# A hybrid encoder block: router in fp32 with tokens on partitions, norm weights applied at the experts' transposes in four parts, convolution evicted behind its last matmul

## The chip, the core and the metric

The kernel is one program on one core of a Trainium2 chip. The metric is device microseconds of one execution. Before the change the median of three runs is 2157.0 us (2156.89 to 2158.53). One further execution was taken with the hardware profiler; its rows are what the document reads.

## The reference, cut to what matters

One encoder layer on 1024 tokens of 1024 channels, all in float32:

```python
h  = rms_norm(x, norm1_g)
z  = h @ w_in                      # columns: q | k | v (512 each), conv a | b (512 each)
attn = dilated_attention(q, k, v)  # 8 heads of 64, three window patterns mixed by their denominators
u  = a * sigmoid(b)
conv = silu(layer_norm(depthwise_conv(u, width 31) + bias))     # 512 channels
x  = x + concat(attn, conv) @ w_out

h   = rms_norm(x, norm2_g)                       # = x * rsqrt(mean(x*x) + eps) * norm2_g
aff = softmax(h @ w_router)                      # 16 experts
gate, idx = top_k(aff.T, 128)                    # each expert chooses its 128 tokens
ye  = (silu(h[idx] @ w1) * (h[idx] @ w3)) @ w2   # per expert, inner width 2816
x   = x + scatter_add(gate * ye, idx)
```

The change touches the depthwise convolution, the second norm with the router, and the place where norm2_g is multiplied in.

## The kernel before, in words

**Number format.** Most products are made of three matmuls in a reduced fp32 format (fp32r in the rows): an operand is split into a high half, rounded on ScalarE, and a low half, the rest, which VectorE or GpSimd subtracts. High times high, high times low and low times high are then summed in PSUM.

**Stages in order.** Until 60 us: loads, the first norm and its splits. 60 to 145 us: the projections for the convolution's two inputs (`z_ab`) and three of the four convolutions. 145 to 300: the projections of q, k and v (`z_pair`, L503), with the fourth convolution at 156 to 171 us. 300 to 447: attention. 447 to 589: the token stage, which makes the output projection, the second norm, the router and the ranking for one block of 128 tokens after another. 589 to 622: the end of the ranking, the search for each expert's tokens, and the first gather. From 622 to the end: sixteen experts of some 94 us each.

**Order of the work.** Each engine works through its own queue in the order in which the kernel issues instructions (`manual_schedule` keeps that order for VectorE, TensorE and ScalarE from the projections to the end). Generators hold back small work and are advanced by hand between other instructions: the ranking's operations are dripped into the token stage, so many at each place, and the glu and the weights' splits are advanced between the convolution's chunks. An instruction that waits holds up what is queued behind it on its engine.

**A convolution** (`conv`) handles 128 of the 512 channels. Its 9 chunks of 4 products with a 128x128 weight run on TensorE over four quarter tiles `ps[:, g]` of 256 columns; one product is three matmuls, and they stand at L362 to L364. Nine products in a row belong to one quarter, so the quarters 0 and 1 are complete in chunk 4. `left(pair)` is ScalarE's eviction of two quarters into the tile `co` with the bias (L341); `to_tokens(pair)` is four 128x128 pieces turned by TensorE into the tile `ct`, then two ScalarE copies into `xn`, tokens on partitions. There is only one `co`, for two quarters, so `left(1)` has to come behind `to_tokens(0)`'s transposes. Before, `left(0)` stands in chunk 4, `to_tokens(0)` at the end of chunk 7, `left(1)` at the end of chunk 8, and `to_tokens(1)` is put in the list `ends`, which `end()` empties between the two parts of the next `z_ab`, or behind the next `z_pair`. Behind the fourth convolution VectorE makes its statistics (`conv_stats`, L377), issued after the token pair that follows, and then rotary rotations and the low halves of the next weights (L407), all in one queue.

**The token stage** (class `Token`, the loop `for t in range(1, NT)`). For a block t: 48 products (`product`) give the output projection, `residual` (L1075, VectorE) adds x, `squares` (L1081, ScalarE) makes the sum of squares, `turned` (L1086) turns the block into eight 128x128 tiles of the transposed x, four in a PSUM tile. ScalarE copies that tile twice: rounded, as the high half, and (L1094) in full into `xf`; GpSimd makes the low half by subtraction (L1095). In the last block VectorE subtracts straight from PSUM. `norm` (L127 to L136) is twelve small VectorE operations for the reciprocal root. `router` (L1116) multiplies with the router's weights as the stationary operand: 128 rows by 32 columns (16 high, 16 low), 128 tokens moving, 16 matmuls into `pr`, experts on partitions. ScalarE copies it to `lT`, `logits` turns it back to tokens on partitions, and VectorE adds the two halves. `softmax` scales by the norm (a ScalarE exponential with a per-token scale), `spread` turns the affinities (L1158) and copies them into the ranking's tile `top`. `kept` makes h for the gather: ScalarE multiplies x by the norm (L1106), GpSimd multiplies by norm2_g, spread over the partitions (`g2`, L1107), and a DMA writes the block to `h2s` in DRAM. The router's weights already hold norm2_g (`router_weights`), so the products take x and not h. The ranking is VectorE's: MAX8 and MATCH_REPLACE runs, then maxima and minima of two SBUF tiles (L989, L991 in `merged`).

**The experts.** For an expert, 128 gathered rows of h (`gather`, an indirect DMA of GpSimd, issued at chunk `GC`) are turned by TensorE (`transposed`, L1417, eight 128x128 pieces in two PSUM tiles) into `xTe`: ScalarE copies a 512-wide tile as the high half (L1419), VectorE subtracts the low half (L1420). That is done at once behind chunk 4 of the expert before. An expert has six chunks of its inner width; each takes two weight tiles for w1, two for w3, and two for w2 (`up`, `down`; the last chunk is half as wide), and each tile is split ahead of use, high half on ScalarE (L1198) and low half on VectorE (L1199). Three high and three low buffers let the splits run three tiles ahead. The products of the chunk before are turned in `h_turned` (L1441).

Of the kernel before, what the change touches and what calls it, by code (L numbers as in the profile page):

```python
# [22 lines left out]
P = 128  # L23
# [4 lines left out]
NE = 16  # L28
# [40 lines left out]
def build(ctx, tc, nc, I, out):  # L69
# [76 lines left out]
    wrr = pack[:, 2 * P:3 * P].rearrange("p (j e) -> p j e", j=8)  # L146
    wr = sm([P, 8, 2, NE], F32R, "wr")
    V.memset(zeros[:, 0, 0:1], 0.0)
# [20 lines left out]
    def router_weights():  # L169
        V.tensor_tensor(wrr, wrr, g2t[:, :, None].to_broadcast([P, 8, NE]), op=ALU.mult)  # L170
        split(wrr, wr[:, :, 0], wr[:, :, 1])

# [161 lines left out]
    def conv(i, ends):  # L334
# [103 lines left out]
    def end():  # L438
        while ends:
            ends.pop(0)()  # L440
# [11 lines left out]
    for i in range(1, 4):  # L452
# [13 lines left out]
        end()  # L466
        z_ab(i, pab, ((1, 1),))
        gates = glu(i, pab[1])
        if i < 3:
# [471 lines left out]
    for n in range(NU + 1):  # L941
# [17 lines left out]
        if n % 4 == 0 and 1 <= h < H - 1:  # L959
# [6 lines left out]
    HW = D + NE  # L966
    misc = slot(4, [D + 2 * P + NT + 2 * NE + 5 * P], F32, "misc")
    g2 = misc[:, 0:D]
    nc.sync.dma_start(g2, I["g2"].partition_broadcast(P))
    cs = misc[:, D:D + 2 * P + NT + 2 * NE]  # L970
# [4 lines left out]
    W, gt, eq = (misc[:, D + 2 * P + NT + 2 * NE + i * P:][:, 0:P] for i in range(3))  # L975
    run = misc[:, D + 5 * P + NT + 2 * NE:].rearrange("p (a k) -> p a k", a=2)
    h2s = dram.tile([S, HW], F32, name="h2s")
# [53 lines left out]
    h22 = slot(10, [2, HW], F32, "h22")  # L1031

    xf = misc[:, D + 2 * P + NT + 2 * NE:][:, 0:512]
    h2T = slot(11, [2, 8, P], F32R, "h2T")
    ORDER = (0, 1, 4, 5, 2, 6, 7, 3)

    class Token:


        def __init__(self, t):  # L1040
            self.t, self.xt, self.h2, self.h2T = t, xt2[:, t % 2], h22[:, t % 2], h2T
            nc.sync.dma_start(self.xt, x_v[:, t])
# [40 lines left out]
        def turned(self, j0, j1, between=None):  # L1083
            pt, n = psT("hT2"), (j1 - j0) * P
            for j in range(j0, j1):
                T.transpose(pt[:, (j - j0) * P:(j - j0 + 1) * P], self.xt[:, j * P:(j + 1) * P], ident)  # L1086
            hh, hl = (self.h2T[:, i, j0:j1].rearrange("p j t -> p (j t)") for i in range(2))
            A.activation(hh, pt[:, 0:n], AF.Copy)
            if between:
                between()  # L1090
            if self.last:
                V.tensor_tensor(hl, pt[:, 0:n], hh.bitcast(F32), op=ALU.subtract)
            else:
                A.activation(xf[:, 0:n], pt[:, 0:n], AF.Copy)  # L1094
                G.tensor_tensor(hl, xf[:, 0:n], hh.bitcast(F32), op=ALU.subtract)  # L1095

# [8 lines left out]
        def scaled(self):  # L1105
            A.activation(self.h2[:, 0:D], self.xt, AF.Copy, scale=self.r)  # L1106
            G.tensor_tensor(self.h2[:, 0:D], self.h2[:, 0:D], g2, op=ALU.mult)  # L1107

        def router(self, j0=0, j1=8):

            if j0 == 0:
                self.pr = psM("pr")
            for part in range(2):
                for j in range(j0, j1):
                    w_ = wr[:, j].rearrange("p a e -> p (a e)")
                    T.matmul(self.pr[0:2 * NE, 0:P], w_, self.h2T[:, part, j], start=j == 0 and not part,  # L1116
                             stop=j == 7 and part == 1)
            if j1 == 8:
                self.lT = pack[0:2 * NE, (3 + self.t % 2) * P:(4 + self.t % 2) * P]
                A.activation(self.lT, self.pr[0:2 * NE, 0:P], AF.Copy)  # L1120

        def logits(self):
            pl = psM("pl")
            T.transpose(pl[:, 0:2 * NE], self.lT, ident[0:2 * NE, 0:2 * NE])
            self.lg = lg = sm([P, NE], F32, "lg", tag="lg", bufs=2)
            self.sc = sm([P, 4], F32, "rsc", tag="rsc", bufs=2)
            V.tensor_copy(lg, pl[:, 0:NE])
            yield
            V.tensor_tensor(lg, pl[:, NE:2 * NE], lg, op=ALU.add)
            yield  # L1130
            V.tensor_reduce(self.sc[:, 0:1], lg, axis=AX.X, op=ALU.max)

        def softmax(self, between=lambda: None, prev=None):
            sc = self.sc
            af = sm([P, NE], F32, "af", tag="af", bufs=2)
            V.tensor_scalar(sc[:, 1:2], sc[:, 0:1], self.r, -1.0, op0=ALU.mult, op1=ALU.mult)
            A.activation(af, self.lg, AF.Exp, scale=self.r, bias=sc[:, 1:2], accum_out=sc[:, 2:3])
            between()
# [272 lines left out]

    def transposed(e, xe):
        xT = slot(XT[e % 2], [2, 8, P], F32R, "xTe")
        for q in range(2):
            pt = psT("xeT")
            for j in range(4):
                T.transpose(pt[:, j * P:(j + 1) * P], xe[:, (4 * q + j) * P:(4 * q + j + 1) * P], ident)  # L1417
            hh = xT[:, 0, 4 * q:4 * q + 4].rearrange("p j t -> p (j t)")
            A.activation(hh, pt, AF.Copy)  # L1419
            V.tensor_tensor(xT[:, 1, 4 * q:4 * q + 4].rearrange("p j t -> p (j t)"), pt, hh.bitcast(F32),  # L1420
                            op=ALU.subtract)
        G.tensor_copy(gate[:, e:e + 1], xe[:, D + e:D + e + 1])
        return xT

# [98 lines left out]
def layouts(inputs):  # L1523
# [6 lines left out]
    L["g1"] = c(f["norm1_g"].reshape(8, P).T)  # L1530
    L["g2"] = c(f["norm2_g"].reshape(1, D))
    L["g2t"] = c(f["norm2_g"].reshape(8, P).T)
# [65 lines left out]
```

## Time and profile before

| | us |
|---|---|
| median of three runs | 2157.0 (2156.89 to 2158.53) |
| the profiled execution's own time | 2155.56 |
| its span | 2153.8 |
| TensorE busy in the span (PE) | 2078.4, 97% |
| its weight loads (PEld) | 1744.8, 81% |
| VectorE (DVE) | 1748.8, 81% |
| ScalarE (ACT) | 1398.6, 65% |
| GpSimd (POOL) | 216.9, 10% |
| high halves of the experts' weights, L1198 (ACT), 530 of 1913 ns mean | 1006.3 |
| low halves, L1199 (DVE), 530 of 2281 ns mean | 1200.6 |

In the rows an instruction is given as its line, engine, operation, the tile it writes, the tile it reads, and the two shapes (partitions x elements). `<-DVE xt L1075` behind an idle time or a wait names what ended it: VectorE's write of the tile `xt` at line 1075. PEld is TensorE's loading of weights, which runs beside its matmuls. The busy share is a mean over stages with different limits, so stretches are read one by one. The chain of waits is followed back from the last instruction of the span, at each step to what released it.

### The profile page before, as it was taken

The page shows a single profiled execution, that of the slowest core. Times are in us where ns is not written, and L with a number is a line of the kernel's source. Part 1 is how long each engine was busy: PE and PEld are TensorE (multiplying, and loading weights), DVE is VectorE, ACT ScalarE, POOL GpSimd, SP SyncE. Part 2 cuts the span into 40 slices and gives each one's busy share as a digit, 9 for nine tenths or more (in the row PEclk, how much of TensorE's full clock was granted, in tenths as well). Part 3 has the DMA queues.
Part 4 walks back from the last instruction along what each step waited for, and adds up shares of the span by engine and source line. Part 5 has one row for each costly group of instructions (what it writes and reads, how often), then busy time and mean ns, then how long its engine had stood idle before and what let it go on. Part 6 is the DMA issues. An engine that isn't in the chain of part 4 may idle for free.

```text
span 2153.8 us, 27850 instructions
## 1 busy us (share of the span) xinstructions
PE 2078.4 (97%) x10458; PEld 1744.8 (81%) x10458; DVE 1748.8 (81%) x2235; ACT 1398.6 (65%) x1463; POOL 216.9 (10%) x164
## 2 busy tenths in 40 slices
PE   9999999998769999999999999999999999999997
PEld 7888889976558888888888888888888888888886
DVE  6346737869968888898898889889888888988885
ACT  5245745553347777777777777777777777777774
POOL 2110001333210100011010101101010100101010
PEclk9999999999979999999999999999999999999998
DMA  8461077744569999999999999999999999999990
GB/s 301 113 170 42 18 170 157 161 141 167 208 248 348 368 386 380 380 375 371 384 363 386 380 380 377 372 380 363 390 378 381 378 368 380 362 388 378 375 354 10
DMA packets 138743, 647.71 MB, mean 301 GB/s; under 512 B 47984, under 2 KB 52464, under 8 KB 68592
## 3 DMA queue, kind: packets, MB, share of 16 engines
q1 hardware_dynamic: 130688, 617.48, 76.9%
q0 software_dynamic: 7776, 28.45, 4.8%
q8 instruction: 82, 1.34, 0.2%
q14 instruction: 53, 0.43, 0.1%
q10 hardware_dynamic: 144, 0.00, 0.0%
HBM read 607.69 MB, written 21.40 MB: 292 GB/s over the span
## 4 chain that ended last, share of the span: by engine, by line
PE 84%; DVE 6%; issue 1%; ACT 1%; DMA 1%; POOL 0%; POOLq 0%; DVEq 0%; ACTq 0%
PE w L113 15%; PE w L115 15%; PE w L114 15%; PE y L115 8%; PE y L113 7%; PE y L114 7%; PE pqk L503 4%; PE po L837 2%; PE pv L503 2%; PE hT L1441 2%; PE pp L817 1%; PE sc L778 1%; DVE top L991 1%; PE sc L779 1%; DVE top L989 1%
## 5 line engine op out<-in xcount | busy, mean ns | idle before, releaser
L1199 DVE TENSOR_TENSOR w<-rw,w 128x2048 fp32r<-128x2048 f32 (+1 forms) x530 | 1200.6, 2281 | 185.0 <-ACT w L1198 180.8
L1198 ACT ACTIVATE w<-rw 128x2048 fp32r<-128x2048 f32 (+1 forms) x530 | 1006.3, 1913 | 274.8 <-PE w L115 138.9
L113 PE MATMUL w<-w,xTe 128*128 128x512 f32 (+1 forms) x1536 | 584.4, 380 | 0.0
L115 PE MATMUL w<-w,xTe 128*128 128x512 f32 (+1 forms) x1536 | 574.8, 374 | 0.0
L114 PE MATMUL w<-w,xTe 128*128 128x512 f32 (+1 forms) x1536 | 574.4, 374 | 0.0
L115 PEld LDWEIGHTS w<-w,xTe 128*128 128x128 f32 x1536 | 289.1, 188 | 54.6 <-DVE xTe L1420 0.2
L114 PEld LDWEIGHTS w<-w,xTe 128*128 128x128 f32 x1536 | 289.8, 189 | 51.5
L113 PEld LDWEIGHTS w<-w,xTe 128*128 128x128 f32 x1536 | 289.4, 188 | 51.1 <-ACT xTe L1419 0.4
L115 PE MATMUL y<-w,hts 128*128 128x512 f32 x700 | 276.8, 395 | 0.0
L113 PE MATMUL y<-w,hts 128*128 128x512 f32 x700 | 275.4, 393 | 0.0
L114 PE MATMUL y<-w,hts 128*128 128x512 f32 x700 | 275.0, 393 | 0.0
L114 PEld LDWEIGHTS y<-w,hts 128*128 128x128 f32 x700 | 131.9, 188 | 30.7
L113 PEld LDWEIGHTS y<-w,hts 128*128 128x128 f32 x700 | 131.9, 188 | 29.1
L115 PEld LDWEIGHTS y<-w,hts 128*128 128x128 f32 x700 | 131.8, 188 | 29.2
L1443 ACT ACTIVATE hts<-hT 128x512 fp32r<-128x512 f32 x95 | 53.8, 566 | 112.5 <-PE hT L1441 112.5
L1477 POOL DMA_INDIRECT out_dram<-xy,idx x16 | 74.4, 4651 | 422.8 <-DVE xy L1476 343.4
L1408 POOL DMA_INDIRECT xy<-h2s,idx x16 | 17.6, 1102 | 895.3 <-PE xeT L1417 683.3
L503 PE MATMUL pqk<-wqkv,hT 128*128 128x512 f32 x384 | 89.6, 394 | 0.0
L503 PEld LDWEIGHTS pqk<-wqkv,hT 128*128 128x128 f32 x384 | 72.1, 188 | 16.5
L164 DVE TENSOR_TENSOR wc<-wcraw,wc 128x512 fp32r<-128x512 f32 x36 | 26.0, 733 | 63.7 <-ACT wc L163 63.7
L837 PEld LDWEIGHTS po<-VAB,pT 128*128 128x128 f32 x496 | 60.5, 195 | 5.3 <-DVE pT L821 2.7
L837 PE MATMUL po<-VAB,pT 128*128 128x65 f32 x496 | 60.6, 276 | 4.2 <-DVE pT L821 2.1
(270 smaller groups left out, 2294.2 us busy)
## 6 DMA issues: line engine op xcount, KB each, us to landing
rw<-in_w SPq DMA_DIRECT2D x525, 1024.0 KB, 7.3
wcraw<-in_wconv POOLq DMA_DIRECT2D x36, 256.0 KB, 4.3
KK<-stg SPq DMA_DIRECT2D x16, 512.0 KB, 6.8
rawqkv<-in_w_qkv SPq DMA_DIRECT2D x6, 1024.0 KB, 4.9
h2s<-h SPq DMA_DIRECT2D x8, 520.0 KB, 2.7
xr<-in_xT SPq DMA_DIRECT2D x8, 512.0 KB, 8.4
xs<-in_x SPq DMA_DIRECT2D x4, 1024.0 KB, 8.6
U<-st SPq DMA_DIRECT2D x64, 64.0 KB, 4.5
```

The source lines that it names most:

```text
L113: T.matmul(ps, xh, wh, start=start, stop=False)
L114: T.matmul(ps, xh, wl, start=False, stop=False)
L115: T.matmul(ps, xl, wh, start=False, stop=stop_)
L164: V.tensor_tensor(lo, raw, hi.bitcast(F32), op=ALU.subtract)
L503: T.matmul(ps[:, k], hT[j][:, a % 2, tok], w[j // 2][:, a // 2, j % 2], start=j == 0 and a == 0, stop=j == 7 and a == 2)
L778: T.matmul(ps[:, i, c], q, kh, start=True, stop=False)
L837: T.matmul(po[:, i * VW:(i + 1) * VW], pt[:, i, c], v, start=c == 0, stop=c == 1)
L1198: A.activation(wh, raws[i][:, c0:c1], AF.Copy)
L1199: E.tensor_tensor(wl, raws[i][:, c0:c1], wh.bitcast(F32), op=ALU.subtract)
L1441: T.transpose(pt[:, k * P:(k + 1) * P], h[:, k * P:(k + 1) * P], ident)
L1443: A.activation(hh, pt[:, 0:w], AF.Copy)
L1477: G.indirect_dma_start(out=out[:, :], out_offset=bass.IndirectOffsetOnAxis(ap=idx[:, e:e + 1], axis=0), in_=ys, in_offset=None, compute_op ...
```

## The change

Three parts.

The convolution: the eviction `left(0)` is issued behind the last matmul, and `to_tokens(0)` with `left(1)`, and `to_tokens(1)`, become two items of the list `ends`. `end()` takes one item per call. It is called between the two parts of `z_ab` and behind them, and `z_pair` calls it between its first two parts and its third where it has two stretches (tp = 0).

The router: one fp32 copy of the transposed x replaces the two halves, with the 128 tokens as the stationary operand and the 16 columns of fp32 router weights moving, so that the logits come out with tokens on partitions and stay in PSUM for the maximum and the exponential. The split of the router's weights, `xf`, GpSimd's subtractions, the copy `lT`, its transpose and the addition go. `h2T` is held twice, once per token parity.

The norm weights: h is stored without norm2_g, so GpSimd's multiplication and the broadcast tile `g2` go. In the experts, `transposed` now takes two pieces at a time, behind chunks 2, 3, 4 and 5 (all four parts in a row ahead of the first expert); ScalarE evicts each piece with norm2_g as a per-partition scale, and VectorE makes the low half by one operation that multiplies and subtracts.

```diff
-            if c == 4:
-                left(0)
-            if c == 7:
-                to_tokens(0)
-            if c == 8:
-                left(1)
             yield
-        ends.append(partial(to_tokens, 1))
+        left(0)
+
+        def half_way():
+            to_tokens(0)
+            left(1)
+
+        ends.extend((half_way, partial(to_tokens, 1)))
...
     def end():
-        while ends:
+        if ends:
             ends.pop(0)()
...
         z_ab(i, pab, ((1, 1),))
+        end()
...
-    def z_pair(ps, tp, w):
+    def z_pair(ps, tp, w, between=lambda: None):
...
+            if 2 not in parts_:
+                between()
...
-            z_pair(ps, tp, w)
+            z_pair(ps, tp, w, end)
             end()
...
     def router_weights():
         V.tensor_tensor(wrr, wrr, g2t[:, :, None].to_broadcast([P, 8, NE]), op=ALU.mult)
-        split(wrr, wr[:, :, 0], wr[:, :, 1])
...
-    g2 = misc[:, 0:D]
-    nc.sync.dma_start(g2, I["g2"].partition_broadcast(P))
...
-    h2T = slot(11, [2, 8, P], F32R, "h2T")
+    h2T = slot(11, [2, 8, P], F32, "h2T")
...
-            hh, hl = (self.h2T[:, i, j0:j1].rearrange("p j t -> p (j t)") for i in range(2))
-            A.activation(hh, pt[:, 0:n], AF.Copy)
+            A.activation(self.h2T[:, j0:j1].rearrange("p j t -> p (j t)"), pt[:, 0:n], AF.Copy)
             if between:
                 between()
-            if self.last:
-                V.tensor_tensor(hl, pt[:, 0:n], hh.bitcast(F32), op=ALU.subtract)
-            else:
-                A.activation(xf[:, 0:n], pt[:, 0:n], AF.Copy)
-                G.tensor_tensor(hl, xf[:, 0:n], hh.bitcast(F32), op=ALU.subtract)
...
             A.activation(self.h2[:, 0:D], self.xt, AF.Copy, scale=self.r)
-            G.tensor_tensor(self.h2[:, 0:D], self.h2[:, 0:D], g2, op=ALU.mult)
...
-            for part in range(2):
-                for j in range(j0, j1):
-                    w_ = wr[:, j].rearrange("p a e -> p (a e)")
-                    T.matmul(self.pr[0:2 * NE, 0:P], w_, self.h2T[:, part, j], start=j == 0 and not part,
-                             stop=j == 7 and part == 1)
-            if j1 == 8:
-                self.lT = pack[0:2 * NE, (3 + self.t % 2) * P:(4 + self.t % 2) * P]
-                A.activation(self.lT, self.pr[0:2 * NE, 0:P], AF.Copy)
+                self.pr = psM("pr")[:, 0:NE]
+            for j in range(j0, j1):
+                T.matmul(self.pr, self.h2T[:, j], wrr[:, j], start=j == 0, stop=j == 7)
...
-            pl = psM("pl")
-            T.transpose(pl[:, 0:2 * NE], self.lT, ident[0:2 * NE, 0:2 * NE])
-            V.tensor_copy(lg, pl[:, 0:NE])
-            V.tensor_tensor(lg, pl[:, NE:2 * NE], lg, op=ALU.add)
-            V.tensor_reduce(self.sc[:, 0:1], lg, axis=AX.X, op=ALU.max)
+            V.tensor_reduce(self.sc[:, 0:1], self.pr, axis=AX.X, op=ALU.max)
...
-            A.activation(af, self.lg, AF.Exp, scale=self.r, bias=sc[:, 1:2], accum_out=sc[:, 2:3])
+            A.activation(af, self.pr, AF.Exp, scale=self.r, bias=sc[:, 1:2], accum_out=sc[:, 2:3])
...
-    def transposed(e, xe):
-        xT = slot(XT[e % 2], [2, 8, P], F32R, "xTe")
-        for q in range(2):
-            pt = psT("xeT")
-            for j in range(4):
-                T.transpose(pt[:, j * P:(j + 1) * P], xe[:, (4 * q + j) * P:(4 * q + j + 1) * P], ident)
-            hh = xT[:, 0, 4 * q:4 * q + 4].rearrange("p j t -> p (j t)")
-            A.activation(hh, pt, AF.Copy)
-            V.tensor_tensor(xT[:, 1, 4 * q:4 * q + 4].rearrange("p j t -> p (j t)"), pt, hh.bitcast(F32),
-                            op=ALU.subtract)
-        G.tensor_copy(gate[:, e:e + 1], xe[:, D + e:D + e + 1])
+    def transposed(e, xe, xT, j0, j1):
+        pt = psT("xeT")
+        for j in range(j0, j1):
+            T.transpose(pt[:, (j - j0) * P:(j - j0 + 1) * P], xe[:, j * P:(j + 1) * P], ident)
+        for j in range(j0, j1):
+            A.activation(xT[:, 0, j], pt[:, (j - j0) * P:(j - j0 + 1) * P], AF.Copy, scale=g2t[:, j:j + 1])
+        for j in range(j0, j1):
+            V.scalar_tensor_tensor(xT[:, 1, j], pt[:, (j - j0) * P:(j - j0 + 1) * P], g2t[:, j:j + 1],
+                                   xT[:, 0, j].bitcast(F32), op0=ALU.mult, op1=ALU.subtract)
+        if j1 == 8:
+            G.tensor_copy(gate[:, e:e + 1], xe[:, D + e:D + e + 1])
...
-    xT = transposed(0, xe)
+    xT = tokens(0)
+    for j in range(0, 8, 2):
+        transposed(0, xe, xT, j, j + 2)
...
-            if c == 4 and e + 1 < NE:
-                xT_next = transposed(e + 1, xe)
+            if 2 <= c and e + 1 < NE:
+                if c == 2:
+                    xT_next = tokens(e + 1)
+                transposed(e + 1, xe, xT_next, 2 * c - 4, 2 * c - 2)
```

## Rows read from the trace of the kernel before

**Rows 1.** Busy us (instructions) of each engine by stretch; granted clock, DMA share

```profile
517.20:534.70 17.50, 15.39 (x74) 11.86 (x74) 16.95 (x94) 5.06 (x12) 7.17 (x6) 0.90 0.47 167
...
552.20:569.90 17.70, 14.16 (x74) 10.63 (x74) 17.14 (x94) 5.05 (x12) 5.36 (x5) 1.00 0.24 91
...
700.00:794.00 94.00, 94.00 (x449) 78.13 (x448) 82.98 (x50) 69.02 (x47) 8.73 (x3) 1.00 0.98 377
```

**Rows 2.** Waits of TensorE, 60:145 and 145:185: total us, times, longest

```profile
PE cv L362 <- ACT pack L341: 4.5, 3, 1.5
...
PE cv L362 <- ACT pack L341: 1.4, 1, 1.4
```

**Rows 3.** Timeline, 72:75: start, us, engine, line, operation, [idle before]

```profile
72.27 0.28 PE L364 MATMUL cv<-U,wc 128*128 128x256 f32 x1
...
74.05 0.39 PE L362 MATMUL cv<-U,wc 128*128 128x256 f32 x1 [1.50 <-ACT pack L341]
```

**Rows 4.** Chain of waits, 0:260: start, us, what

```profile
182.98 66.73 PE pqk L503 x288
```

**Rows 5.** Timeline of VectorE, 165:262

```profile
190.87 0.69 DVE L377 BATCH_NORM_STATS2 bst<-xn 128x6 f32<-128x512 f32 x1
...
203.84 1.22 DVE L407 TENSOR_TENSOR wqkv<-rawqkv,wqkv 128x1024 fp32r<-128x1024 f32 x1
...
209.82 2.35 DVE L407 TENSOR_TENSOR wqkv<-rawqkv,wqkv 128x1024 fp32r<-128x1024 f32 x2
```

**Rows 6.** Groups of GpSimd, 447:600: busy us, mean ns, idle before

```profile
L1107 POOL TENSOR_TENSOR h<-h,misc 128x1024 f32<-128x1024 f32 x8 | 19.0, 2383 | 1.5 <-ACT h L1106 1.5
L1095 POOL TENSOR_TENSOR h2T<-misc,h2T 128x512 fp32r<-128x512 f32 x14 | 18.3, 1308 | 38.6 <-ACT misc L1094 38.3
```

**Rows 7.** Timeline of GpSimd, 540:576

```profile
547.12 2.40 POOL L1107 TENSOR_TENSOR h<-h,misc 128x1024 f32<-128x1024 f32 x1
```

**Rows 8.** Timeline of VectorE, 540:576

```profile
546.03 1.20 DVE L989 TENSOR_TENSOR top<-top 128x64 f32<-128x64 f32 x1
547.16 2.43 DVE L991 TENSOR_TENSOR top<-top 128x64 f32<-128x64 f32 x1
...
549.77 0.22 DVE L991 TENSOR_TENSOR top<-top 128x64 f32<-128x64 f32 x1
...
554.42 1.28 DVE L134 SCALAR_TENSOR_TENSOR rha<-rha,ms 128x1 f32<-128x1 f32 x1
```

**Rows 9.** Timeline of TensorE, 540:576

```profile
555.01 1.15 PE L1116 MATMUL pr<-h2T,wr 128*32 128x128 f32 x16
...
560.10 0.66 PE L1086 MATMUL hT<-ident,xt 128*128 128x128 f32 x4 [0.49 <-DVE xt L1075]
...
563.09 0.33 PE L1158 MATMUL pa<-ident,pack 128*128 128x128 f32 x1 [0.95 <-DVE pack L1146]
...
569.92 0.66 PE L1086 MATMUL hT<-ident,xt 128*128 128x128 f32 x4 [2.10 <-DVE xt L1075]
```

**Rows 10.** Waits of TensorE, 447:500 and 500:576

```profile
PE hT L1086 <- DVE xt L1075: 2.6, 3, 1.2
PE pa L1158 <- DVE pack L1146: 1.1, 1, 1.1
...
PE hT L1086 <- DVE xt L1075: 9.9, 6, 2.6
PE pa L1158 <- DVE pack L1146: 2.6, 2, 1.6
```

**Rows 11.** Chain of waits, whole span: start, us, what

```profile
387.52 1.74 PE po L837 x16
...
702.48 0.88 PE xeT L1417 x8
...
975.07 0.44 PE hT L1441 x4
```

**Rows 12.** Timeline of ScalarE, 690:730

```profile
702.96 1.09 ACT L1419 ACTIVATE xTe<-xeT 128x512 fp32r<-128x512 f32 x2 [1.27 <-PE xeT L1417]
```

More of the change, by code (lines that the diff above doesn't have):

```diff
@@ L146, in build @@
     wrr = pack[:, 2 * P:3 * P].rearrange("p (j e) -> p j e", j=8)
-    wr = sm([P, 8, 2, NE], F32R, "wr")
     V.memset(zeros[:, 0, 0:1], 0.0)
@@ L966, in build @@
     HW = D + NE
-    misc = slot(4, [D + 2 * P + NT + 2 * NE + 5 * P], F32, "misc")
-    g2 = misc[:, 0:D]
-    nc.sync.dma_start(g2, I["g2"].partition_broadcast(P))
-    cs = misc[:, D:D + 2 * P + NT + 2 * NE]
+    misc = slot(4, [2 * P + NT + 2 * NE + 5 * P], F32, "misc")
+    cs = misc[:, 0:2 * P + NT + 2 * NE]
     nc.sync.dma_start(cs, I["places"])
@@ L974, in build @@
                                 (2 * P + NT + NE, 2 * P + NT + 2 * NE)))
-    W, gt, eq = (misc[:, D + 2 * P + NT + 2 * NE + i * P:][:, 0:P] for i in range(3))
-    run = misc[:, D + 5 * P + NT + 2 * NE:].rearrange("p (a k) -> p a k", a=2)
+    W, gt, eq = (misc[:, 2 * P + NT + 2 * NE + i * P:][:, 0:P] for i in range(3))
+    run = misc[:, 5 * P + NT + 2 * NE:].rearrange("p (a k) -> p a k", a=2)
     h2s = dram.tile([S, HW], F32, name="h2s")
@@ L1031, in build @@
     h22 = slot(10, [2, HW], F32, "h22")
-    xf = misc[:, D + 2 * P + NT + 2 * NE:][:, 0:512]
-    h2T = slot(11, [2, 8, P], F32R, "h2T")
+    h2T = slot(11, [2, 8, P], F32, "h2T")
     ORDER = (0, 1, 4, 5, 2, 6, 7, 3)
@@ L1040, in __init__ @@
         def __init__(self, t):
-            self.t, self.xt, self.h2, self.h2T = t, xt2[:, t % 2], h22[:, t % 2], h2T
+            self.t, self.xt, self.h2, self.h2T = t, xt2[:, t % 2], h22[:, t % 2], h2T[:, t % 2]
             nc.sync.dma_start(self.xt, x_v[:, t])
@@ L1106, in scaled @@
             A.activation(self.h2[:, 0:D], self.xt, AF.Copy, scale=self.r)
-            G.tensor_tensor(self.h2[:, 0:D], self.h2[:, 0:D], g2, op=ALU.mult)
         def router(self, j0=0, j1=8):
             if j0 == 0:
-                self.pr = psM("pr")
-            for part in range(2):
-                for j in range(j0, j1):
-                    w_ = wr[:, j].rearrange("p a e -> p (a e)")
-                    T.matmul(self.pr[0:2 * NE, 0:P], w_, self.h2T[:, part, j], start=j == 0 and not part,
-                             stop=j == 7 and part == 1)
-            if j1 == 8:
-                self.lT = pack[0:2 * NE, (3 + self.t % 2) * P:(4 + self.t % 2) * P]
-                A.activation(self.lT, self.pr[0:2 * NE, 0:P], AF.Copy)
+                self.pr = psM("pr")[:, 0:NE]
+            for j in range(j0, j1):
+                T.matmul(self.pr, self.h2T[:, j], wrr[:, j], start=j == 0, stop=j == 7)
         def logits(self):
-            pl = psM("pl")
-            T.transpose(pl[:, 0:2 * NE], self.lT, ident[0:2 * NE, 0:2 * NE])
-            self.lg = lg = sm([P, NE], F32, "lg", tag="lg", bufs=2)
             self.sc = sm([P, 4], F32, "rsc", tag="rsc", bufs=2)
-            V.tensor_copy(lg, pl[:, 0:NE])
             yield
-            V.tensor_tensor(lg, pl[:, NE:2 * NE], lg, op=ALU.add)
             yield
-            V.tensor_reduce(self.sc[:, 0:1], lg, axis=AX.X, op=ALU.max)
+            V.tensor_reduce(self.sc[:, 0:1], self.pr, axis=AX.X, op=ALU.max)
         def softmax(self, between=lambda: None, prev=None):
@@ L1410, in gather, with tokens @@
         return xe
-    def transposed(e, xe):
-        xT = slot(XT[e % 2], [2, 8, P], F32R, "xTe")
-        for q in range(2):
-            pt = psT("xeT")
-            for j in range(4):
-                T.transpose(pt[:, j * P:(j + 1) * P], xe[:, (4 * q + j) * P:(4 * q + j + 1) * P], ident)
-            hh = xT[:, 0, 4 * q:4 * q + 4].rearrange("p j t -> p (j t)")
-            A.activation(hh, pt, AF.Copy)
-            V.tensor_tensor(xT[:, 1, 4 * q:4 * q + 4].rearrange("p j t -> p (j t)"), pt, hh.bitcast(F32),
-                            op=ALU.subtract)
-        G.tensor_copy(gate[:, e:e + 1], xe[:, D + e:D + e + 1])
-        return xT
+    def transposed(e, xe, xT, j0, j1):
[9 more added lines that the diff above has]
+            G.tensor_copy(gate[:, e:e + 1], xe[:, D + e:D + e + 1])
+    def tokens(e):
+        return slot(XT[e % 2], [2, 8, P], F32R, "xTe")
     def width(c):
@@ L1530, in layouts @@
     L["g1"] = c(f["norm1_g"].reshape(8, P).T)
-    L["g2"] = c(f["norm2_g"].reshape(1, D))
     L["g2t"] = c(f["norm2_g"].reshape(8, P).T)
```

## Prediction

> **What bounds the kernel now.** I read the span by stages first. In the experts' stage, which begins near 622 us and fills 71% of the span, TensorE is busy for all 94.00 us of a 94 us stretch at full granted clock, with VectorE at 82.98 and ScalarE at 69.02 [rows 1]. There a gain on another engine is worth nothing, and a loss counts only where TensorE must wait. In the stage before it, which makes h, the router and the ranking for one block of 128 tokens after another, one block takes 17.5 to 17.7 us; VectorE is busy for 16.95 to 17.14 of them, TensorE for 14.16 to 15.39, the larger figure at a granted clock of 0.90 [rows 1]. So VectorE sets that pace. In the convolutions TensorE sets the pace and stands still at one place only.
>
> Durations are from the profiled execution: span 2153.8 us, its own time 2155.56. The median of the three runs, 2157.0, is 1.4 us above it.
>
> **Step 1, the convolution evicted behind its last matmul.** TensorE waits 4.5 us in three convolutions and 1.4 in the fourth for ScalarE's eviction of the first two quarter tiles [rows 2]. The last matmul ahead of it starts at 72.27, matmuls follow each other every 0.12 us, and the next starts at 74.05 [rows 3]: 74.05 - 72.39 = 1.66 us. Four times about 1.63 is 6.5 us. Behind the last matmul the same eviction lies beside 24 products of the next projection (24 x 0.232 = 5.6 us at the 66.73 us for 288 of rows 4), and the transposes then find it done. Without that cover each would cost the 1.66 us again.
>
> One thing becomes late. In the last convolution the transposes are now spread over two places: the second half comes behind the token pair that starts at 182.98, not ahead of it [rows 4]. That pair takes 48 x 0.232 = 11.12 us, so the transposes end at 194.54 and ScalarE's copies let VectorE's first convolution statistics start at about 195.0. Now they start at 190.87 [rows 5]. VectorE takes its queue in order, so the rotation and the low halves of the next weights behind them move by 4.1 us. The last two low halves run from 209.82 for 2.35 us [rows 5] and would end near 215.1 and 216.3. TensorE wants them after 32 + 8 and 32 + 12 products of the pair that starts at 182.98 + 2 x 11.12 + 0.44 = 205.66, at 214.9 and 215.9. So it loses about 0.5 us (0 if the copies land earlier, 2 at most: the third weight would then be late too). Step 1 gives 6.0 us, bounds 4.0 and 6.8.
>
> **Step 2, the router and GpSimd's part of the token stage.** Two kinds of GpSimd operation vanish: 14 subtractions of 1308 ns and 8 multiplications by g2 of 2383 ns [rows 6]. Their own time is off the path, but while one runs, VectorE's operations with two operands in SBUF do not finish: with the multiplication that starts at 547.12 for 2.40 us [rows 7], the VectorE comparison at 547.16 takes 2.43 us; the same comparison takes 0.22 at 549.77 [rows 8]. One block has three such places: 1.20, 2.43 and 1.28 us where 0.22 each is usual [rows 8], so 4.91 - 0.66 = 4.25 us. VectorE's period falls from 17.7 to 13.4. (The two small operations that join the logits' halves go too, some tenths that I leave out.)
>
> What is late next is TensorE. Its period: 48 products x 0.232 = 11.1, 8 transposes 0.9 [rows 11], the router now 16 matmuls from 555.01 in about 1.0 [rows 9], two small transposes 0.3: 13.3. The fp32 router has 8 matmuls with 128 tokens as weights and 16 columns. No row has this shape. The nearest is the fp32 product of attention, 128x128 weights and 65 columns: 16 in 1.74 us, 0.109 each with its load [rows 11]. That bounds it from above at 8 x 0.109 = 0.87 us; below, at a quarter of that. I take 0.87, and the transpose of the logits and its eviction vanish: 13.0, and with 0.4 for restarts behind waits 13.4. Two engines of 13.4 that hand work to each other wait now and then: I take 13.7. Three like periods, 17.5, 17.5 and 17.7, save 3.8 + 3.8 + 4.0 = 11.6.
>
> For the other blocks I count TensorE's waits. From 447 to 576 us it waits 2.6 and 9.9 us for the residual ahead of its transposes and 1.1 and 2.6 for the ranking's input [rows 10], 16.2 in all. Three are 0.49, 0.95 and 2.10 [rows 9], and each of the two periods before has one like the last: 7.7 lie in the three periods. The 8.5 left, in the earlier blocks, go nearly whole: 8.0. In the last block VectorE loses one GpSimd place (1.0) and its own three subtractions of low halves (some 1.5): 2.5. Step 2 gives 11.6 + 8.0 + 2.5 = 22 us. Above: all 16.2, some 3.5 that two periods lose at a granted clock of 0.90 (two times a tenth of 17.5), 0.3 of TensorE work for each of 8 blocks and the 2.5: 25. Below: half of it, 11, if the two engines keep waiting for each other. The ends of the ranking, the search and the first gather behind it are not touched.
>
> The Trainium skill speaks against the fp32 router here. Its page FP8 and Floating Point Precision, section TensorE Precision Notes, gives true fp32 four passes, and TensorE: Matmul & The Clock Gate, section LDWEIGHTS, makes a load as long as its 128 columns, 107 ns whatever the matmul. If each pass loaded anew, the estimate by these pages is 8 x 4 x 0.107 = 3.4 us, 2.4 more than now. The 0.109 us of the attention product leaves no room for four loads.
>
> **Step 3, the experts' transposes in four parts.** The PE work: eight transposes take 0.88 on the chain and four of the other kind 0.44 [rows 11], so the price goes with the number and two should take 0.22. Bounds for the 15 experts: 0, and 13 us if a part of two costs as much as a group of four (4 x 0.44 - 0.88 = 0.88 each). I take 0.5. ScalarE now evicts two 512-wide tiles in 1.09 us after an idle 1.27 [rows 12], with the next weight split behind them; TensorE loses nothing by it [rows 1]. A part has two 128-wide evictions with a scale operand, between a quarter and the whole of 0.55 us each, so at most the same 1.09, four times per expert. ScalarE has 25 us to spare in 94, VectorE 11, against some 1 to 2 more on either. The cover is the three weight tiles split ahead: the split behind a part must be done within two tiles of 12 x 0.232 and the small transposes, about 6.2 us, and needs about 1.2 for the part, 1.9 on ScalarE and 2.3 on VectorE (the two groups that head the page's list): 5.4. The gather of the next expert leaves later, behind the last part, but is not wanted before chunk 2 of the next expert. Ahead of the first expert all four parts run with two PSUM buffers, so the third waits for evictions: 0.3 (0 to 1.5). Step 3 costs 0.8, bounds 0 and 14.
>
> The dropped split of the router's weights and the g2 load lie beside attention and other loads: 0.
>
> **Sum.** 6.0 + 22 - 0.8 = 27.2 us. The profiled execution would take 2155.6 - 27.2 = 2128.4, a run 1.4 more: 2130 us.
>
> **Rivals.**
> A. The engines of the token stage wait in turn and keep half of what VectorE gains: 6 + 11 - 0.8 = 16, 2141 us. For it: the handovers of rows 9 come at four places per block. Against: VectorE's queue holds ranking work that fills such waits.
> B. Slower: the parts break the cover in the experts. One place, ScalarE's queue: a part's evictions stand ahead of the next split, and with 60 parts each must cost TensorE more than 28 / 60 = 0.47 us for the kernel to lose. If one costs 0.6, 28 - 36 gives 2165 us. It decides when evictions and split together exceed 6.2 us, that is 0.8 above my 5.4; for it, that margin is thin; against, the block of today is as long and costs nothing.
> C. The fp32 router loads four times: +2.4 us in each of 7 blocks on a TensorE that then sets the pace, 27 - 17 = 10, 2147 us. Rows 11 speak against it.
> D. The convolution's wait only moves to the transposes behind the next projection: 27 - 6 = 21, 2136 us. Against: 5.6 us of cover for an eviction of under 2.
>
> **How the numbers follow.** Forecast 0.70 (its own range 2123 to 2138), A 0.13, B 0.06, C 0.05, D 0.06. The range 2121 to 2143 holds the forecast with the upper bound of step 2, A and D, and leaves out B, C and a tail of A. A measurement tells 0.2%, 4.3 us. Faster by more: all but most of B and slivers of the others, 0.93; within it 0.02; slower 0.05.
>
> **What would show it.** Step 1: no wait of TensorE for ScalarE inside a convolution, and the first statistics about 4 us later against the token pair. Step 2: no VectorE comparison above 0.3 us between 480 and 575, block periods of 13 to 14.5 us, the clock at 1.00 there. Step 3: TensorE busy through 94 to 95 us per expert. If the periods stay above 16 us, the GpSimd lock was not the price; if an expert takes 97 us or more, step 3 was wrong.

## The result, and the profile after

The changed kernel takes 2133.26 us, median of four runs (2133.21 to 2135.30), against 2157.77 (2156.89 to 2160.06) of the kernel before beside it: ratio 0.9886, 95% interval 0.9874 to 0.9898, so 24.5 us faster. The forecast was 2130 with a range of 2121 to 2143. Timed again in another session, the same program took 2138.52 (2137.91 to 2139.46; ratio 0.9912, 0.9895 to 0.9928). Nearly all of the 5 us between the two lies ahead of the token stage's second router, where TensorE's granted clock was lower; the rows at the end of the next section show where. The profiled execution took 2133.22 us, span 2131.4, so 22.3 us less than that of before.

The page's totals after:

```profile
PE 2076.2 (97%) x10450; PEld 1745.7 (82%) x10450; DVE 1738.8 (82%) x2311; ACT 1407.6 (66%) x1536; POOL 165.9 (8%) x142
```

Of the totals only GpSimd's differs much from before (165.9 us for 216.9); the stages do. Where the 22.3 us lie, from the same event in both traces:

| stretch | before | after | difference |
|---|---|---|---|
| to the end of the last product of v | 296.42 | 290.23 | -6.2 |
| from there to the first product of the token stage | 151.35 | 150.80 | -0.55 |
| token stage, to TensorE's products ahead of the first gather | 163.78 | 145.35 | -18.4 |
| from there to the first product of an expert | 10.28 | 11.38 | +1.1 |
| from that product to the end of the span | 1531.97 | 1533.64 | +1.7 |

The convolutions first. TensorE's waits in the changed kernel from 55 to 300 us; the four of [rows 2] are gone, and one of 0.3 us for a low half of weights is new:

```profile
PE pp L818 <- ACT SP L809: 2.1, 1, 2.1
PE pqk L502 <- DVE wqkv L405: 0.3, 1, 0.3
```

Then one block of the token stage, as in [rows 1], by stretch (busy us of PE, PEld, DVE, ACT, POOL; granted clock, DMA share, GB/s):

```profile
504.94:518.85 13.91, 13.91 (x74) 11.65 (x73) 13.32 (x98) 4.46 (x10) 1.74 (x3) 1.00 0.73 263
518.85:532.74 13.89, 13.89 (x74) 11.67 (x73) 13.27 (x97) 4.08 (x9) 0.38 (x2) 1.00 0.34 124
...
677.59:771.59 94.00, 94.00 (x449) 77.93 (x448) 83.66 (x56) 69.72 (x54) 9.23 (x3) 1.00 0.98 376
```

A block takes 13.9 us instead of 17.5, and the bound has changed hands: TensorE is busy throughout, VectorE for 13.3 in these two and for 12.8 in the third. The granted clock is 1.00 in both, where the first block of [rows 1] had 0.90. In the experts (last row) TensorE is as full as before. VectorE's comparisons, which answer to [rows 8], all take their usual time, 0.28 us at most between 440 and 590:

```profile
524.81 0.23 DVE L988 TENSOR_TENSOR top<-top 128x64 f32<-128x64 f32 x1
524.95 0.22 DVE L990 TENSOR_TENSOR top<-top 128x64 f32<-128x64 f32 x1
```

And TensorE's router, as in [rows 9]:

```profile
549.37 1.85 PE L1104 MATMUL pr<-pack,h2T 128*128 128x16 f32 x16
```

The eight matmuls of the code stand as 16 rows here. In the chain of waits they take 1.69 us; the next product starts at 551.07.

### The profile page after: what moved, and what is told of

The parts are those of the page before. It is cut to its first block, busy times and chain, and to the rows that moved or that the text cites. A ratio compares the mean times of both kernels' runs of the same rounds, so it can differ in the third digit from the quotient of the medians.

```text
span 2131.4 us, 27950 instructions
## 1 busy us (share of the span) xinstructions
PE 2076.2 (97%) x10450; PEld 1745.7 (82%) x10450; DVE 1738.8 (82%) x2311; ACT 1407.6 (66%) x1536; POOL 165.9 (8%) x142
## 4 chain that ended last, share of the span: by engine, by line
PE 93%; DVE 4%; DMA 1%; ACT 1%; issue 1%; POOLq 0%; SPq 0%; POOL 0%; DVEq 0%; ACTq 0%
PE w L113 15%; PE w L115 15%; PE w L114 15%; PE y L115 8%; PE y L114 8%; PE y L113 8%; PE wo L1067 4%; PE pqk L502 3%; PE po L838 2%; PE pv L502 2%; PE hT L1423 2%; PE pp L818 1%; PE sc L779 1%; PE sc L780 1%; PE cv L362 1%; PE cv L360 1%
## 5 line engine op out<-in xcount | busy, mean ns | idle before, releaser
L1387 POOL DMA_INDIRECT xy<-h2s,idx x16 | 23.2, 1450 | 1079.2 <-PE xeT L1395 820.2
L1397 ACT ACTIVATE xTe<-xeT,g2t 128x128 fp32r<-128x128 f32 x128 | 39.9, 365 | 80.4 <-PE xeT L1395 80.4
L1459 POOL DMA_INDIRECT out_dram<-xy,idx x16 | 63.4, 3964 | 258.4 <-DVE xy L1458 179.0
```

Of the source, the lines that this page charges most:

```text
L1397: A.activation(xT[:, 0, j], pt[:, (j - j0) * P:(j - j0 + 1) * P], AF.Copy, scale=g2t[:, j:j + 1])
L1459: G.indirect_dma_start(out=out[:, :], out_offset=bass.IndirectOffsetOnAxis(ap=idx[:, e:e + 1], axis=0), in_=ys, in_offset=None, compute_op ...
```

## The experiments

Each run is compared with the kernel before, timed on the same chip in the same session (2157.96, 2158.18 and 2158.66 us in the three).

**The convolution alone.** The kernel before with the convolution's hunks of the diff, from `left(0)` to `z_pair`, and nothing else.

> The kernel before with the convolution's edit alone (left(0) behind the last matmul, two items in ends). Theory: the waits in the convolutions, 5.9 us, go, and the last product of v ends 6.2 us earlier, as it does in the changed kernel (290.23 against 296.42), and nothing behind it gives that back: 6 us less than before, some 2151. Rival, given back: what follows the projections is set by loads or by attention's own chain, and the time stays within 2 us of before, 2156.

2151.98 us (2149.84 to 2152.81; ratio 0.9969, 0.9957 to 0.9981): 6.0 us. The last product of v ends at 290.17. The gain holds to the end; the rival falls.

**GpSimd's multiplication put back**, the router as changed:

```diff
             A.activation(self.h2[:, 0:D], self.xt, AF.Copy, scale=self.r)
+            G.tensor_tensor(self.h2[:, 0:D], self.h2[:, 0:D], g2, op=ALU.mult)
...
-            A.activation(xT[:, 0, j], pt[:, (j - j0) * P:(j - j0 + 1) * P], AF.Copy, scale=g2t[:, j:j + 1])
+            A.activation(xT[:, 0, j], pt[:, (j - j0) * P:(j - j0 + 1) * P], AF.Copy)
...
```

> The changed kernel with GpSimd's multiplication by norm2_g back in kept() and the experts' evictions in the same four parts without a scale. Theory (VectorE's operations with two SBUF operands stand still while GpSimd's operation runs): VectorE's 13.3 us per block become 13.3 + (2.43 - 0.22) + (1.20 - 0.22) = 16.5, over TensorE's 13.9, so each of the three like blocks gets 2.6 us longer and the earlier ones somewhat: 8 to 12 us slower than the changed kernel, 2141 to 2145, with comparisons of about 2.4 and 1.2 us in the trace. Rival (GpSimd's work costs only its own engine, the gain came from the router's shorter chain): 2133 to 2134, block periods of 13.9.

2142.85 us (2140.12 to 2144.85; ratio 0.9928, 0.9914 to 0.9942). The rival falls: eight multiplications on an engine that is mostly idle cost 4 to 10 us, by which of the two timings of the changed kernel it is held against. Per block, GpSimd, then the one VectorE comparison under it, then TensorE's transposes one block apart:

```profile
535.32 2.40 POOL L1100 TENSOR_TENSOR h<-h,misc 128x1024 f32<-128x1024 f32 x1 [0.53 <-ACT h L1099]
```

```profile
535.44 2.36 DVE L990 TENSOR_TENSOR top<-top 128x64 f32<-128x64 f32 x1
```

```profile
532.33 0.60 PE L1085 MATMUL hT<-ident,xt 128*128 128x128 f32 x4
540.17 0.66 PE L1085 MATMUL hT<-ident,xt 128*128 128x128 f32 x4 [1.04 <-DVE xt L1074]
547.79 0.60 PE L1085 MATMUL hT<-ident,xt 128*128 128x128 f32 x4
```

The period is 15.46 us, not the 16.5 that I expected. I had charged two stalls to the multiplication; the second, of 1.20 us, is a subtraction's. With one, 13.3 + 2.36 - 0.22 = 15.44. The 13.3 in this sum is a period, not a busy time. The block from 532.33 by stretch, columns as above:

```profile
532.33:547.79 15.46, 14.32 (x74) 11.50 (x73) 14.87 (x93) 3.78 (x8) 2.76 (x3) 1.00 0.28 103
```

VectorE is busy for 14.87 us, so for 12.73 without the stall; no wait of it is listed, and the other 0.59 lie between its instructions. 12.73 + 0.59 gives 13.3. That it is busy for 13.3 in two blocks of the changed kernel is a coincidence: those hold four or five instructions more.

**The norm weights alone**: the kernel before without the multiplication, `transposed` as changed; GpSimd's subtractions, the old router and the old convolution stay.

> The kernel before with norm2_g moved to the experts' transposes in four parts, alone: GpSimd's multiplication goes, its subtractions and the router of before stay, the convolution as before. Theory of the lock: a block loses 3.2 of its 4.25 us of stalls, 17.6 becomes 14.4, three like blocks save 9.5 us, the earlier ones some 4, and the experts cost 2.8 (1.2 ahead of the first, 1.7 behind): 2157 - 11 = 2146. Rival (the multiplication is hidden, the gain of the change is the router's): 2157 + 2.8 = 2160.

2150.79 us (2148.50 to 2151.91; ratio 0.9963, 0.9950 to 0.9977), 7.2 us faster where 11 were expected; the rival falls. The two stalls that are left, both under subtractions of some 1.3 us (VectorE):

```profile
528.49 1.21 DVE L987 TENSOR_TENSOR top<-top 128x64 f32<-128x64 f32 x1
...
534.87 1.12 DVE L136 SCALAR_TENSOR_TENSOR rhr<-rha,rhr 128x1 f32<-128x1 f32 x1
```

13.3 + (1.21 - 0.22) + (1.12 - 0.14) = 15.27; the period is 15.28 (540.18 to 555.46). The like blocks got 6.7 us shorter together (46.03 from 517.02 to 563.05) where I had 9.5: the same wrong attribution as above. The earlier blocks got 0.3 shorter (69.18 from 447.84) where I had some 4. TensorE's granted clock was 0.91 to 0.93 from 448 to 490 us in this profile and 1.00 in that of before; how much of the 4 it took is open.

**What in GpSimd's work blocks VectorE.** Three runs add work to each block of the changed kernel that nothing reads: two copies, two memsets, and the memsets again, held in place by a manual schedule of GpSimd. Each edit cut to its main lines, in this order (`scr` is a new part of the tile `misc`):

```diff
             A.activation(self.h2[:, 0:D], self.xt, AF.Copy, scale=self.r)
+            for _ in range(2):
+                G.tensor_copy(scr, self.h2[:, 0:D])
```

```diff
             A.activation(self.h2[:, 0:D], self.xt, AF.Copy, scale=self.r)
+            for _ in range(2):
+                G.memset(scr, 0.0)
```

```diff
+            with tc.manual_schedule(engines={mybir.EngineType.Pool}):
...
+                for _ in range(2):
+                    G.memset(scr, 0.0)
```

> The changed kernel with two GpSimd copies of h (128x1024, one operand in SBUF each) into a tile that nothing reads, added to kept(). Theory from this case (VectorE's operations with two SBUF operands stand while GpSimd reads SBUF, whatever the GpSimd operation): one comparison per copy takes as long as the copy, VectorE's 13.3 us per block grow by the copies' time less 0.2 each, and periods pass 13.9 once the copies exceed some 1 us together. With 1 us each: 14.9, 5 to 8 us slower than the changed kernel, 2140. The Trainium skill, page SBUF - State Buffer, section Who interferes with whom, says the same: the conflict is with a GpSimd instruction that reads SBUF. Rival (only GpSimd operations with two SBUF operands do it): 2133.

> The changed kernel with two GpSimd memsets of a 128x1024 tile that nothing reads, added to kept(). If GpSimd's reading is what blocks VectorE, these cost nothing: 2133, periods of 13.9, and no comparison over 0.3 us. Rival (any GpSimd operation on SBUF blocks VectorE's operations with two operands): comparisons of about 1 us beside each memset and 2138 to 2140. The Trainium skill, page SBUF - State Buffer, section Who interferes with whom, speaks for the first.

> The changed kernel with two GpSimd memsets of a 128x1024 tile that nothing reads behind each block's copies, held in that place (in the run pool_write they ran ahead of the ranking, from 437 to 458 us, and met no comparison). Each takes 0.955 us there. If only GpSimd's reading blocks VectorE, periods stay 13.9 and no comparison passes 0.3 us: the time of the run of the changed kernel beside it. Rival (any GpSimd operation on SBUF): comparisons of about 0.95 us beside them, periods of 14.7 as with the copies, 5 to 8 us slower.

The copies: 2141.63 us (2139.09 to 2142.37). GpSimd and VectorE:

```profile
536.74 2.16 POOL L1100 COPY misc<-h 128x1024 f32<-128x1024 f32 x2 [0.59 <-ACT h L1098]
```

```profile
536.79 1.06 DVE L989 TENSOR_TENSOR top<-top 128x64 f32<-128x64 f32 x1
538.03 0.94 DVE L989 TENSOR_TENSOR top<-top 128x64 f32<-128x64 f32 x1
```

13.3 + 0.84 + 0.72 = 14.86, and the period is 14.90 (533.67 to 548.57). So one operand in SBUF on GpSimd's side is enough. The first memsets decide nothing: with no operand to wait for they ran between 437.8 and 458.3 us, ahead of the ranking, among GpSimd's splits of w_out's weights (2137.17 us). Held in place, 2135.70 us (2133.14 to 2138.47), within the two timings of the changed kernel. GpSimd, and VectorE's comparisons under the same memsets:

```profile
532.69 1.97 POOL L1136 MEMSET misc<- 128x1024 f32 x2
```

```profile
533.00 0.23 DVE L989 TENSOR_TENSOR top<-top 128x64 f32<-128x64 f32 x1
533.14 0.22 DVE L991 TENSOR_TENSOR top<-top 128x64 f32<-128x64 f32 x1
...
534.33 0.22 DVE L991 TENSOR_TENSOR top<-top 128x64 f32<-128x64 f32 x1
```

Twelve comparisons run at 0.21 to 0.27 us between 532.56 and 534.95, and the period is 13.88. GpSimd's reading of SBUF blocks, its writing does not. The Trainium skill, page SBUF — State Buffer, section Who interferes with whom, states just that: a VectorE instruction with two SBUF inputs contends with a GpSimd instruction that reads SBUF, not with one that only writes it. These traces agree: 0.94 to 2.43 us instead of 0.22 with reads, 0.21 to 0.27 with writes.

**The router in one pass**, to price the fp32 router.

```diff
+    wr = sm([P, 8, NE], F32R, "wr")
...
+        A.activation(wr, wrr, AF.Copy)
...
-    h2T = slot(11, [2, 8, P], F32, "h2T")
+    h2T = slot(11, [2, 8, P], F32R, "h2T")
...
-                T.matmul(self.pr, self.h2T[:, j], wrr[:, j], start=j == 0, stop=j == 7)
+                T.matmul(self.pr, self.h2T[:, j], wr[:, j], start=j == 0, stop=j == 7)
```

> The changed kernel with tokens and router weights rounded to fp32r, so one matmul per product (it leaves out the low halves). Theory (TensorE sets the pace of 13.9 us, and the fp32 router's 1.69 us are on it): the router takes 0.85, TensorE's period falls to 13.05, VectorE's 13.3 is the next bound, periods of 13.4: 3 x 0.5 for the like blocks, up to 0.8 for each of four earlier ones, 0.4 in the last: 2133.3 - 2.5 to 5, about 2129.5. Rival (VectorE sets the pace already, or the 16 rows are no more work than 8): 2133, periods of 13.9.

```profile
537.77 0.95 PE L1106 MATMUL pr<-wr,h2T 128*128 128x16 f32 x8
```

Eight rows now, 0.95 us of modelled length instead of 1.85. The three like blocks by stretch, columns as above:

```profile
507.94:521.75 13.81, 13.19 (x66) 10.68 (x65) 13.22 (x97) 4.34 (x10) 1.75 (x3) 1.00 0.73 267
521.75:535.03 13.28, 13.23 (x67) 10.69 (x65) 12.69 (x92) 3.90 (x9) 0.37 (x2) 1.00 0.33 119
535.03:548.29 13.26, 13.19 (x66) 10.69 (x65) 12.67 (x92) 3.88 (x9) 0.37 (x2) 1.00 0.33 122
```

They were 13.91, 13.89 and 13.87. So the fp32 router was on the path. With the 0.6 us between its instructions VectorE is the next bound: its 13.22 make 13.8 and its 12.7 make 13.3. In the two short blocks TensorE has under 0.1 us to spare, so there the two engines are level.

The time, 2133.77 us (2132.09 to 2134.13), shows less: the stretch from 457 to 475 us had a granted clock of 0.91, and the first block's transposes start at 461.97, not 459.51. By the time alone the run is inconclusive. By its stages it is not. The changed kernel's second profile has the same granted clock as this one, 0.97 from the start of the token stage to the like blocks and 1.00 in them. There the token stage takes 146.90 us (444.37 to 591.27), here 143.07 (443.49 to 586.56): 3.8 us less, inside the 2.5 to 5 expected. By parts that is 1.0 in the earlier blocks, 1.3 in the like ones and 1.5 behind.

**The experts' transposes, all at once.**

```diff
-            if 2 <= c and e + 1 < NE:
-                if c == 2:
-                    xT_next = tokens(e + 1)
-                transposed(e + 1, xe, xT_next, 2 * c - 4, 2 * c - 2)
+            if c == 4 and e + 1 < NE:
+                xT_next = tokens(e + 1)
+                for j in range(0, 8, 4):
+                    transposed(e + 1, xe, xT_next, j, j + 4)
```

> The changed kernel with the experts' transposes in two groups of four behind chunk 4, with the scaled 128-wide evictions, also ahead of the first expert. Theory of the prediction's cover: 8 evictions of 0.365 us stand ahead of the next split, 2.9 + 1.9 + 2.3 = 7.1 us against 6.2, so TensorE loses up to 0.9 us for each of 15 experts, less about 1.5 us gained ahead of the first expert: 2133 + 12 = 2145. Rival (three tiles of splits ahead hide that too, so the four parts buy nothing): 2133 - 1.5 - 0.9 = 2131.

2137.47 us (2136.37 to 2139.48; ratio 0.9905, 0.9890 to 0.9920), between the two timings of the changed kernel. The price per expert is read from GpSimd's scattered stores, one per expert; their starts in the kernel before, the changed one, and all at once:

```profile
826.93 3.39 POOL L1477 DMA_INDIRECT out_dram<-xy,idx  x1 [18.12 <-DVE xy L1476]
921.93 5.59 POOL L1477 DMA_INDIRECT out_dram<-xy,idx  x1 [18.17 <-DVE xy L1476]
```

```profile
803.71 3.39 POOL L1459 DMA_INDIRECT out_dram<-xy,idx  x1 [6.56 <-DVE xy L1458]
898.72 3.40 POOL L1459 DMA_INDIRECT out_dram<-xy,idx  x1 [6.56 <-DVE xy L1458]
```

```profile
805.69 3.39 POOL L1459 DMA_INDIRECT out_dram<-xy,idx  x1 [18.00 <-DVE xy L1458]
900.93 3.39 POOL L1459 DMA_INDIRECT out_dram<-xy,idx  x1 [18.01 <-DVE xy L1458]
```

The intervals alternate between two values, before 94.50 and 95.00, after 94.63 and 95.02, all at once 94.73 and 95.23. Over before, four parts cost 0.13 and 0.02 in turn (1.1 us for 15 experts), all at once 0.23 each (3.4 us). My reckoning of the cover, 0.9 each, was wrong in its place. ScalarE's eight evictions run into each other (2.17 us, not 2.9) and the splits hold. What comes late is the low half of the next product's operand behind VectorE's eight subtractions. VectorE, then TensorE, all at once:

```profile
777.18 2.16 DVE L1399 SCALAR_TENSOR_TENSOR xTe<-xeT,g2t,xTe 128x128 fp32r<-128x128 f32 x8
780.02 2.29 DVE L1178 TENSOR_TENSOR w<-rw,w 128x2048 fp32r<-128x2048 f32 x1 [0.68 <-ACT w L1177]
782.23 0.69 DVE L1426 TENSOR_TENSOR hts<-hT,hts 128x512 fp32r<-128x512 f32 x1
```

```profile
782.63 0.39 PE L114 MATMUL y<-w,hts 128*128 128x512 f32 x1
782.97 0.50 PE L115 MATMUL y<-w,hts 128*128 128x512 f32 x1
783.31 0.40 PE L113 MATMUL y<-w,hts 128*128 128x512 f32 x1
```

`hts` is complete at 782.92. The product that reads it starts 0.34 us after the one ahead, and so does the next, instead of 0.23 each: 0.22 lost, with no wait named, since the rows' modelled lengths cover it. In the kernel before the subtractions took 1.28 us and nothing was late.

**The first expert's transposes in two groups of four**, the rest as changed.

```diff
-    for j in range(0, 8, 2):
-        transposed(0, xe, xT, j, j + 2)
+    for j in range(0, 8, 4):
+        transposed(0, xe, xT, j, j + 4)
```

> The changed kernel with the first expert's transposes in two groups of four instead of four of two; the later experts as in the changed kernel. Theory: between the gather's landing and the first product the changed kernel takes 3.09 us (594.67 to 597.76), of which 1.12 us is the wait for a PSUM tile; with two groups it takes 1.70, as in the run with all groups of four, and the first products at half clock are 4 and not 8, 0.75 us: 2133.3 - 2.1 = 2131. Rival (the first products are held by their weights anyway): 2133.

> The changed kernel unaltered, as the other side of the two runs beside it: 2133 to 2135, since TensorE's granted clock in the stretch from 440 to 480 us was 0.91 in some executions and 1.00 in others, about 3 us apart.

> The changed kernel with the first expert's transposes in two groups of four, a second time, beside the changed kernel on the same chip. Theory: 2.1 us less than the run beside it (1.4 ahead of the first product, 0.75 at the half clock). Rival: no difference.

The changed kernel, then this one, from the gather's landing:

```profile
594.67 1.12 PE L1395 MATMUL xeT<-ident,xy 128*128 128x128 f32 x4 [4.09 <-DMA xy<-h2s,idx]
596.91 1.21 PE L1395 MATMUL xeT<-ident,xy 128*128 128x128 f32 x4 [1.12 <-DVE xTe L1399]
597.76 0.78 PE L113 MATMUL w<-w,xTe 128*128 128x512 f32 x1
```

```profile
597.64 1.97 PE L1395 MATMUL xeT<-ident,xy 128*128 128x128 f32 x8 [4.21 <-DMA xy<-h2s,idx]
599.34 0.79 PE L113 MATMUL w<-w,xTe 128*128 128x512 f32 x1
```

1.70 us instead of 3.09, and the first store comes 112.34 us behind the landing instead of 114.40 (597.64 to 709.98; 594.67 to 709.07): 2.06, as expected. Landing to the end of the span is 1533.3 us in both profiles of this version, 1536.7 and 1537.1 in the two of the changed kernel; 1.4 of that lies in the last expert, where the code is the same. There TensorE waits 2.5 us for the last `sg`, and behind that wait its clock differs. The last 15 us ahead of the last store, in the changed kernel, then here:

```profile
2106.59:2121.59 15.00, 11.09 (x46) 8.73 (x45) 6.16 (x6) 3.74 (x5) 0.00 (x0) 0.89 0.00 0
```

```profile
2106.06:2121.06 15.00, 11.08 (x58) 9.03 (x57) 7.23 (x8) 5.18 (x7) 0.00 (x1) 1.00 0.00 0
```

The granted clock is 1.00 in both profiles of this version and 0.89 in the eleven others, the kernel before among them; in the changed kernel's first profile six products behind the wait start 0.43 us apart, at the lower level of 1.2 GHz, and the rest 0.23. Whether the edit brings that about is not shown. In time: 2133.05 (2129.45 to 2134.62) and 2133.60 (2131.66 to 2133.82), the second beside the changed kernel's 2138.52 in the same session. Ratios to before are 0.9879 (0.9862 to 0.9895) and 0.9885 (0.9869 to 0.9902). It is the best version here by its traces, 2.1 us by the edit; of the 4.9 us in that session no more than that is shown to be the edit's.

That clock, in the profile of the changed kernel's second timing, then in its first (columns as above):

```profile
420.00:440.00 20.00, 17.60 (x131) 17.15 (x130) 15.45 (x43) 13.82 (x29) 9.40 (x5) 0.89 0.60 185
440.00:460.00 20.00, 19.33 (x93) 16.38 (x91) 11.60 (x19) 5.65 (x9) 4.75 (x2) 0.94 0.18 64
460.00:480.00 20.00, 18.39 (x92) 14.82 (x91) 9.37 (x36) 9.28 (x17) 0.35 (x2) 0.91 0.42 145
```

```profile
420.00:440.00 20.00, 17.43 (x148) 16.64 (x147) 16.07 (x44) 14.63 (x30) 10.69 (x5) 1.00 0.58 179
440.00:460.00 20.00, 18.18 (x81) 14.28 (x81) 12.61 (x20) 4.61 (x7) 2.75 (x2) 1.00 0.16 53
460.00:480.00 20.00, 19.16 (x114) 16.37 (x113) 12.27 (x79) 10.77 (x19) 0.35 (x2) 1.00 0.43 159
```

One program, and the first product of the token stage starts at 444.37 against 441.03. Of these 3.3 us 0.8 are there by 414 us, most likely from the stretch from 300 to 320, where the granted clock was 0.93 against 0.98. Another 1.6 us go between the first router and the second (466.79 to 481.42, against 463.45 to 476.45). From the second router on the two run alike to 0.4 us: 13.9 us a block, 94.63 and 95.02 an expert.

## Why the prediction was right, and where it was off

| step | predicted | profiled executions |
|---|---|---|
| 1, convolution | -6.0 (4.0 to 6.8) | -6.2; alone, by time, -6.0 |
| 2, token stage | -22 (11 to 25) | -18.4 |
| 3, experts | +0.8 (0 to 14) | +2.8 |
| sum | -27.2 | -22.3, with -0.55 in attention that I had not counted |

**Step 1** came out as worked out. The waits went, the statistics start 11.98 us behind their token pair (175.61 to 187.59, the pair's start by the chain of waits as in [rows 4]) where it was 7.89, so 4.1 later, as predicted, and the stall was 0.3 where I had 0.5. Rival D falls: the transposes behind the next projection wait for nothing.

**Step 2** had the right mechanism and one term mis-sized. The mechanism: a GpSimd operation that reads SBUF holds up VectorE's operations with two SBUF operands. Put back, left in or replaced, every such operation lengthened the period by its stall less 0.22 us, to within 0.05 us in three kernels. The mis-sized term is the fp32 router: 0.87 us predicted, 1.69 measured. I read 16 rows of [rows 11] as 16 products of 0.109 us. The loop in `products` issues 8 matmuls there, so a fp32 product stands as two rows and takes 0.22. My upper bound for the router was therefore half of what those rows say. TensorE's 13.0 became 13.9, which happens to be near the 13.7 that I had set for two engines waiting on each other; they do not wait, TensorE is simply full, and that the period came near is luck. So the three like blocks gave 11.0 of the 11.6 (517.21 to 569.92 against 504.94 to 546.61). The earlier blocks gave 5.5 of the 8.0 (447.77 to 517.21 against 441.03 to 504.94). The last block gave 1.9 of 2.5. The run in one pass shows what the term is worth, since half of 1.69 is nearly the 0.87 that I had: its token stage is 3.8 us shorter at the same granted clock, and 18.4 + 3.8 is the 22 predicted. By parts it is not so even. The earlier blocks get 1.0 of that, so 1.5 of their missing 2.5 stay open, and the like blocks, with 1.3, come out better than I had reckoned. Rival A falls with the full TensorE. Rival C had the right instinct and too high a price. The Trainium skill's four passes (page FP8 and Floating Point Precision, section TensorE Precision Notes) gave an estimate of 3.4 us with a new load for each; the trace shows 16 loads and 16 rows for the 8 products, two of each. I was right to take less than that and wrong to take a quarter.

**Step 3** was small, as said, but 2.8 and not 0.8. Ahead of the first expert the wait for the second pair of PSUM buffers is 1.12 us, where I had 0.3, and the pause leaves 8 first products at the lower clock of 1.2 GHz (starts 0.43 us apart, not 0.23) where it was 4 (0.75). The other 15 experts cost 1.1, where I had 0.5. Rival B falls, and its reckoning too: with all eight evictions at once the splits still came in time, and the loss of 0.23 us an expert was VectorE's.

## What to carry to other kernels

Price an idle engine's work by what it holds up elsewhere: look under its operations for rows of another engine that take four to ten times their usual length, and charge each such place to the one operation that covers it. Before a duration is taken from a group of rows, count the instructions that the code issues there. When a bound is lifted, work out the next engine's period from its own rows and expect that engine to be full, not the two to wait in turn.

## What the runs showed of the hardware that was not expected

A fp32 matmul with 128 tokens as weights and 16 columns costs 0.21 us, two rows with a load each; rounded to fp32r it is one row, and with eight rows fewer two of the three like blocks are 0.6 us shorter. GpSimd's memset of 128x1024 (0.955 us) leaves VectorE's comparisons at 0.22 us, its copy of the same size stretches one to 0.94 to 1.06. A VectorE operation with one operand in its row is not held up: beside GpSimd's 1.90 us from 504.43 (L1276, changed kernel) each MATCH_REPLACE8 takes its usual 0.21. TensorE's granted clock between 420 and 480 us was 0.89 to 0.94 in one profile of the changed kernel and 1.00 in the other, though TensorE's longest wait there was alike (2.02 and 2.03 us, for `attnT` at L894); the two timings of that program are 5.3 us apart. In the last 15 us ahead of the last store it was 0.89 in eleven profiles and 1.00 in two, behind the same wait of 2.5 us. What decides was not found in either place.
